# Gates of two token blocks written into a zeroed DRAM table by accumulating indirect DMAs, instead of through one-hot products

## The chip, the cores and the metric

One core of one Trainium2 chip runs the whole program. Its engines are TensorE (PE, with PEld for the weight load beside it), VectorE (DVE), ScalarE (ACT), GpSimd (POOL) and SyncE (SP). Plain DMAs are issued by SP, indirect ones by POOL. The metric is the device time of one execution in microseconds (us).

## The reference, cut to what matters

A decoder block over 1024 tokens of 1024 numbers, in float32: a gated DeltaNet and a sliding-window attention side by side, an output projection, a PEER layer (product-key retrieval of single-neuron experts), a gated input embedding and a last norm. The change is in the PEER layer. Each token and each of 8 heads picks 16 of 16,384 experts, with softmax gates:

```
qry = (ht @ wq).reshape(T, PEER_HEADS, 2, PEER_KEY_DIM)
sc = jnp.einsum("thpd,hpnd->thpn", qry, sub_keys)
top_s, top_i = lax.top_k(sc, K)                       # K = 16
cand_s = top_s[:, :, 0, :, None] + top_s[:, :, 1, None, :]
cand_i = top_i[:, :, 0, :, None] * PEER_N_KEYS + top_i[:, :, 1, None, :]
best_s, best_pos = lax.top_k(cand_s.reshape(T, PEER_HEADS, K * K), K)
expert = jnp.take_along_axis(cand_i.reshape(T, PEER_HEADS, K * K), best_pos, axis=-1)
gates = jax.nn.softmax(best_s, axis=-1)
act = jax.nn.gelu(jnp.einsum("td,thkd->thk", xb, u_tab[eb]))
y = jnp.einsum("thk,thkd->td", gb * act, v_tab[eb])
```

## The kernel before

The 1024 tokens are eight blocks of 128. Blocks 0 to 4 are computed densely: every expert's row of `u` and `v` passes through TensorE for all 640 tokens, and a table of gates (zero where an expert was not picked) multiplies the activations. Blocks 5 to 7 gather the picked rows instead: per block 128 indirect DMAs of 128 rows of 4 KB from `u` and 128 from `v` (L854), with a dot product or a multiply-add on VectorE for each.

`upstream()` (L325) comes first. `project` runs once for each half of the sequence (norm, input projection, convolution). Then, group by group of two blocks (`GROUPS`, L28), `mixers` computes DeltaNet and attention, and `retrieve` computes the output projection, the norm, the queries, the scores against the sub-keys, the first top-k (`first_topk`) and the second (`topk`). The norm's factor `rs` is computed by two small POOL instructions (`rs_v` L154, `rs` L155) that the norm on VectorE (`h<-x,rs,ffn_norm`) waits for; the DeltaNet output's factors `ro` and `rq` take the same two lines, and the attention's padded keys and values (`kz`, `vz`) are prepared on POOL too.

At the end of `topk` of a dense block, `gbuild` (L832) builds the block's part of the gate table: for four tokens at a time, VectorE compares an index row with `iota` twice (tiles `o1` and `o2`, shown as `o`), ScalarE scales by the gates, TensorE multiplies (`bk_gm`), ScalarE copies to `stage`, and 1 MB at a time goes to the DRAM table `gd` (L849), 40 stores in all. Every token block takes 64 one-hot comparisons.

`dense()` (L920) then takes the 128 rows of experts in groups of four (`cg`): it loads the group's gates into `Gt` (L965), multiplies the token parts by `u` (`bk_u`, parts of 320 + 320 tokens), applies Gelu, multiplies by the gates (`ge<-ge,Gt`), and sums the products with `v` (`bk_y`, `bk_yp`). Beside it a paced job issues the gathers of blocks 5 to 7, its VectorE work tied to the progress of the dense stage (`held_back`). `final()` ends the program. The pool `gp` of the gather buffers is opened at L352, inside `upstream`, the pool `gx` after it.

The order on each engine is set before the run, by a scheduler that simulates the program; on the chip each engine runs that order and waits where a semaphore says so. SP and POOL too issue their DMAs in that order.

Of the kernel before, what the change touches and what calls it, by code (L numbers as in the profile page):

```python
# [6 lines left out]

F32 = mybir.dt.float32
F32R = mybir.dt.float32r
BF = mybir.dt.bfloat16  # L10
I32 = mybir.dt.int32
# [18 lines left out]
DBLK = [0, 1, 2, 3, 4]  # L30
ABLK = [5, 6, 7]
# [3 lines left out]
GC = 4  # L35
# [10 lines left out]
def _consts():  # L46
    import numpy as np

    r = np.arange(P)
    parts = [np.eye(P), r[:, None] <= r[None, :], r[:, None] > r[None, :], np.ones((P, P)),  # L50
             np.broadcast_to(r[None, :], (P, P)), r[None, :] > r[:, None]]
    for l in range(7):
        s = 1 << l
        same = (r[:, None] // (2 * s)) == (r[None, :] // (2 * s))
        low = same & (r[:, None] % (2 * s) >= s) & (r[None, :] % (2 * s) < s)
        parts.append(low if l == 0 else low.T[:, r % (2 * s) >= s])
    sel = np.zeros((P, 8 + 50 + 16 + 16 + 16))
    sel[:, :8] = (500000.0 ** (-np.arange(0, 16, 2) / 16)).astype(np.float32)
    widths = [16 // (a + 1) for a in range(16)]
    starts = np.concatenate([[0], np.cumsum(widths)[:-1]])  # L60
    sel[:, 58:74] = starts
    sel[:, 74:90] = np.concatenate([[0], np.diff(starts)])
    sel[:, 90:106] = np.arange(16)
    return np.concatenate([np.concatenate(parts, axis=1), sel], axis=1).astype(np.float32)
# [3 lines left out]
def block_kernel(ctx: ExitStack, tc, I, out, dbg=None):  # L68
# [56 lines left out]
    negt = c2.tile([P, 1], F32, name="negt")  # L125

    def load_consts():
        nc.sync.dma_start(ident, I["consts"][:, 0:P])
        nc.sync.dma_start(cst, I["consts"][:, P:])
        V.tensor_copy(sel_b.rearrange("p s a h -> p (s a) h"), bc(sel[:, 58:106], 2, 8))  # L130
        V.memset(negt, NEG)

# [14 lines left out]
    gd = dr.tile([NE // GC, P, NT // TB, GC, TB], F32, name="gd")  # L147

    eidx = cp.tile([P, len(UBLK), P], I32, name="eidx")
# [71 lines left out]
    def project(hf, es):  # L221
# [30 lines left out]
        for ct in range(12):  # L252
            wh, wl = weights(I["wc"][ct], [P, DK, P])
            if hf:
                for i in range(2 * ct, 2 * ct + 2):
                    cached_tile(i)
            raw = sm.tile([P, 3 + H], F32, tag="craw", name="craw")
# [67 lines left out]
    def upstream():  # L325
        with early as em:
# [25 lines left out]
            pools["gp"] = ctx.enter_context(tc.tile_pool(name="gp", bufs=GBUF, side="right", reuse_waits="tile"))  # L352
# [29 lines left out]
    def retrieving(lt, es):  # L382
# [14 lines left out]
        def retrieve(gi):  # L397
# [62 lines left out]
            for bi, b in enumerate(grp):  # L460
                topk(lt, bg, b, tv[bi], tiu[bi])
                if b in HBLK:
                    pools["job"] = half_job()
                tick(2.0)

# [286 lines left out]
    def topk(tk, bg, b, v, iu):  # L752
# [52 lines left out]
        ga = gate_a[:, UBLK.index(b)] if b in UBLK else flat[:, 2 * P:3 * P]  # L805
# [9 lines left out]
        if b in ABLK:  # L815
            return
# [13 lines left out]
    slots = {}  # L830

    def gbuild(bg, b):  # L832
        tT = slots[b]
        for tb in range(P // TB):
# [14 lines left out]
            nc.sync.dma_start(gd[:, :, BBLK.index(b) * (P // TB) + tb].rearrange("g p c t -> p g (c t)"),  # L849
# [70 lines left out]
    def dense(xB):  # L920
        with ExitStack() as es:
# [12 lines left out]
            nparts = (NU + 511) // 512  # L934
            width = (NU // nparts + TB - 1) // TB * TB
            parts = [(n0, min(width, NU - n0)) for n0 in range(0, NU, width)]
# [26 lines left out]
            for cg in range(NE // GC):  # L963
                Gt = ap.tile([P, NT // TB, GC, TB], F32, tag="Gt", name="Gt", bufs=1)
                nc.sync.dma_start(Gt, gd[cg])  # L965
                vs, ws = [], []
                for ci in range(GC):
# [10 lines left out]
                    for n0, n in parts:  # L978
# [6 lines left out]
                        g3 = ge.rearrange("p (t k) -> p t k", k=TB)  # L985
                        m0 = NH + n0
                        tt(g3, g3, Gt[:, m0 // TB:(m0 + n) // TB, ci, :], ALU.mult)
# [76 lines left out]
    upstream()  # L1064
    pools["gx"] = ctx.enter_context(tc.tile_pool(name="gx", bufs=GXBUF, side="right", reuse_waits="tile"))
# [63 lines left out]
```

## Time and profile before

| | |
|---|---|
| median of 3 runs | 3067.3 us (3066.24 to 3071.76) |
| profiled execution | 3063.47 us |
| its span | 3061.7 us |
| mean granted TensorE clock | 0.982 |
| PE busy | 2943.6 us, 96% of the span |
| DVE busy | 2527.3 us, 83% |
| ACT busy | 1232.8 us, 40% |
| POOL busy | 1092.6 us, 36% |
| moved by DMA | 869.27 MB, mean 284 GB/s |

The profile shows busy time of each engine, and idle time with what ended it. Register and semaphore instructions and the issuing of plain DMAs are not counted as busy; an indirect DMA's issue on POOL is. "Landing" is the time from a DMA's issue to its last byte. Each row of a stage view tells busy time and number of instructions per engine, the granted clock as a share of full speed, and the mean share of the core's 16 DMA engines in use.

### The profile page before, as it was taken

The numbers are of one execution on the slowest core, as the hardware profiler recorded it, in microseconds if no ns is written. First come the engines' busy times: TensorE is split into PE (matmuls) and PEld (weight loads), VectorE is DVE, ScalarE is ACT, GpSimd is POOL, SyncE is SP. The second block draws the span as 40 slices with busy tenths as digits, with TensorE's granted clock in tenths as the row PEclk, the third lists the DMA queues.
The fourth block names the chain that finished last, engine by engine and source line by source line (L and its number), as shares of the span: only waits on it lengthen the run. The fifth ranks groups of instructions, "written<-read, shape, count | busy, mean of one in ns | idle before, by whom it ended". The sixth has DMA issues, their size and how long they took to land. (4 is left out here: it accounts for less than half of the span.)

```text
span 3061.7 us, 50184 instructions
## 1 busy us (share of the span) xinstructions
PE 2943.6 (96%) x18287; PEld 2694.2 (88%) x18287; DVE 2527.3 (83%) x5327; ACT 1232.8 (40%) x2761; POOL 1092.6 (36%) x901
## 2 busy tenths in 40 slices
PE   7999999999998877999999999999999999999998
PEld 5888999999997877889989989899899899998977
DVE  5658636899999879988899988889888888898984
ACT  5567634477876742322323223223222232222233
POOL 0000000000000001656465565655654665555631
PEclk9999999999999988999999999999999999999999
DMA  6569667778879895999899989989998899899962
GB/s 234 141 237 360 202 212 230 238 230 241 243 226 272 227 289 185 352 339 336 294 357 331 349 325 351 331 319 331 331 325 320 307 340 323 311 347 329 324 231 89
DMA packets 449815, 869.27 MB, mean 284 GB/s; under 512 B 193440, under 2 KB 235680, under 8 KB 445216
## 3 DMA queue, kind: packets, MB, share of 16 engines
q1 hardware_dynamic: 338976, 463.37, 45.6%
q0 software_dynamic: 110592, 402.70, 36.5%
q8 instruction: 144, 2.36, 0.3%
q14 instruction: 103, 0.84, 0.1%
HBM read 766.34 MB, written 99.61 MB: 283 GB/s over the span
## 5 line engine op out<-in xcount | busy, mean ns | idle before, releaser
L134 PE MATMUL bk_u<-hT,uh 128*128 128x320 f32 x4096 | 914.3, 310 | 8.6 <-DMA hT<-h2Td 6.5
L134 PEld LDWEIGHTS bk_u<-hT,uh 128*128 128x128 f32 x4096 | 694.5, 188 | 25.5 <-DMA hT<-h2Td 7.0
L854 POOL DMA_INDIRECT rows<-in_u_dram,eidx x384 | 516.7, 1346 | 539.6 <-DVE dots L864 328.4
L854 POOL DMA_INDIRECT rows<-in_v_dram,eidx x384 | 504.0, 1312 | 374.2 <-DVE acc L82 301.1
L134 PE MATMUL bk_u<-hT,ul 128*128 128x320 f32 x2048 | 634.1, 310 | 0.0
L82 DVE SCALAR_TENSOR_TENSOR acc<-rows,dots,acc 128x1024 f32<-128x1024 f32 x384 | 491.5, 1280 | 16.5 <-DMA rows<-in_v_dram,eidx 7.0
L864 DVE CUSTOM_DVE_ANT_0 rows<-rows,h2n 128x1024 f32<-128x1024 f32 x384 | 457.0, 1219 | 50.1 <-DMA rows<-in_u_dram,eidx 42.4
L134 PEld LDWEIGHTS bk_u<-hT,ul 128*128 128x128 f32 x2048 | 385.6, 188 | 3.3
L984 ACT ACTIVATE ge<-bk_u 128x320 f32<-128x320 f32 x256 | 109.4, 428 | 634.9 <-PE bk_u L134 610.2
L134 PE MATMUL bk_y<-vh,wh 128*128 128x512 f32 x768 | 301.6, 393 | 17.7 <-DVE xB L79 17.0
L134 PE MATMUL bk_y<-vl,wh 128*128 128x512 f32 x768 | 302.6, 394 | 0.0
L134 PE MATMUL bk_y<-vh,wl 128*128 128x512 f32 x768 | 301.0, 394 | 0.5 <-DVE wl L79 0.5
L76 ACT ACTIVATE wh<-ge 128x320 fp32r<-128x320 f32 x256 | 118.9, 469 | 308.4 <-DVE ge L79 270.2
L134 PE MATMUL bk_gm<-o,o 128*128 128x128 f32 x1280 | 203.2, 290 | 33.2 <-ACT o L76 21.0
L76 ACT ACTIVATE o<-o,tT 128x128 f32<-128x128 f32 x640 | 203.5, 392 | 57.9 <-DVE o L79 56.2
L134 PEld LDWEIGHTS bk_gm<-o,o 128*128 128x128 f32 x1280 | 179.5, 199 | 39.7 <-ACT o L76 26.0
L79 DVE TENSOR_TENSOR o<-cst,tT 128x512 f32<-128x512 f32 x320 | 204.7, 682 | 10.9 <-PE bk_gm L134 9.0
L134 PE MATMUL bk_s<-h,whi 128*128 128x256 f32 x1024 | 210.4, 297 | 2.9 <-DMA whi<-wqc 1.6
L76 ACT ACTIVATE vh<-vr 128x1024 fp32r<-128x1024 f32 x128 | 132.0, 1054 | 181.7 <-PE bk_y L134 100.5
L134 PE MATMUL bk_yp<-vh,wh 128*128 128x512 f32 x512 | 199.0, 392 | 2.2 <-ACT wh L76 2.2
L76 ACT ACTIVATE uh<-ur 128x1024 fp32r<-128x1024 f32 x128 | 135.3, 1057 | 160.4 <-PE bk_u L134 143.4
L134 PE MATMUL bk_yp<-vl,wh 128*128 128x512 f32 x512 | 199.5, 392 | 0.0
(302 smaller groups left out, 5861.8 us busy)
## 6 DMA issues: line engine op xcount, KB each, us to landing
ur<-in_uT_dram SPq DMA_DIRECT2D x128, 512.0 KB, 6.9
vr<-in_v_dram SPq DMA_DIRECT2D x128, 512.0 KB, 6.2
gd<-stage SPq DMA_DIRECT2D x40, 1024.0 KB, 7.0
Gt<-gd SPq DMA_DIRECT2D x32, 1280.0 KB, 8.8
wlo<-wqc SPq DMA_DIRECT2D x128, 256.0 KB, 4.4
whi<-wqc SPq DMA_DIRECT2D x128, 256.0 KB, 4.2
whi<-woc SPq DMA_DIRECT2D x64, 256.0 KB, 4.6
wlo<-woc SPq DMA_DIRECT2D x64, 256.0 KB, 4.8
```

The costliest lines, as they stand in the source:

```text
L76: return S.activation(o, i, AF.Copy, **k)
L79: return V.tensor_tensor(o, a, b, op)
L82: return V.scalar_tensor_tensor(o, a, s, b, op0, op1, **k)
L134: PE.matmul(o, l, r, start=start, stop=stop)
L854: G.indirect_dma_start(out=r, out_offset=None, in_=tab, in_offset=bass.IndirectOffsetOnAxis(ap=eidx[:, u, s:s + 1], axis=0))
L864: held_back(V.tensor_tensor_reduce(out=r, in0=r, in1=h2n, op0=ALU.mult, op1=ALU.add, scale=1.0, scalar=0.0, accum_out=dots[:, s:s + 1]))
L984: S.activation(ge, pa, AF.Gelu_apprx_tanh)
```

## The change

Blocks 0 and 1 (`SBLK`) no longer pass through `gbuild`. Their `topk` leaves the gates in `sgate` and an address in `sidx`: expert x 256 + token, the token counted within the two blocks. `scattered()`, called at the end of `retrieve(0)`, issues 8 x 2 x 16 = 256 indirect DMAs from POOL, each of which adds 128 gates (one for each token of a block) to 128 single elements of a second DRAM table, `gsd`, of 4,194,304 elements (16.8 MB). The 16 DMAs of a head carry a dependency on all 16 of the previous head of the same block, so that two heads that pick the same expert for the same token do not overlap. `gsd` is filled with zeros by 16 stores of 1 MB (2 KB pieces, from a zero tile in SBUF) that `project(0)` issues on SP. The table `gd` shrinks to the 384 tokens of blocks 2 to 4, with 24 stores instead of 40; in the dense stage a group loads `Gt` of 768 KB and `Gs` of 512 KB (in 1 KB pieces, from `gsd`) instead of `Gt` of 1280 KB, and the token parts become 256 + 384. The pool `gp` is opened after `upstream()`.

```diff
--- before
+++ after
@@ -28,6 +29,8 @@
 DBLK = [0, 1, 2, 3, 4]
+SBLK = [0, 1]
+NS = len(SBLK) * 128
 ABLK = [5, 6, 7]
@@ -58,6 +61,7 @@
     starts = np.concatenate([[0], np.cumsum(widths)[:-1]])
+    sel[:, 8] = r
     sel[:, 58:74] = starts
@@ -123,12 +127,17 @@
     negt = c2.tile([P, 1], F32, name="negt")
+    zero = c2.tile([P, 512], F32, name="zero")
+    scol = cp.tile([P, len(SBLK)], F32, name="scol")
...
         V.memset(negt, NEG)
+        V.memset(zero, 0.0)
+        for i in range(len(SBLK)):
+            V.tensor_scalar(scol[:, i:i + 1], sel[:, 8:9], float(i * P), None, op0=ALU.add)
@@ -144,8 +153,13 @@
     h2Td = [dr.tile([P, DK, NU], F32, name=f"h2Td{i}") for i in range(2)]
-    gd = dr.tile([NE // GC, P, NT // TB, GC, TB], F32, name="gd")
-
+    NO = NT - NS
+    gd = dr.tile([NE // GC, P, NO // TB, GC, TB], F32, name="gd")
+
+    gsd = dr.tile([NE * P * NS, 1], F32, name="gsd")
+    lanes = dram_disjoint_views(gsd, 16 * len(SBLK))
+    sidx = cp.tile([P, len(SBLK), P], I32, name="sidx")
+    sgate = cp.tile([P, len(SBLK), P], F32, name="sgate")
     eidx = cp.tile([P, len(UBLK), P], I32, name="eidx")
@@ -254,6 +268,10 @@
                     cached_tile(i)
+            if not hf and ct < 8:
+                for z in range(2 * ct, 2 * ct + 2):
+                    zf = gsd.rearrange("(z p n k) o -> z p n (k o)", z=16, p=P, k=512)[z]
+                    nc.sync.dma_start(zf, bc(zero, 1, zf.shape[1]))
             raw = sm.tile([P, 3 + H], F32, tag="craw", name="craw")
@@ -349,7 +367,6 @@
                 project(1, (c1, wp, sm))
-            pools["gp"] = ctx.enter_context(tc.tile_pool(name="gp", bufs=GBUF, side="right", reuse_waits="tile"))
             with ExitStack() as es:
@@ -459,9 +476,9 @@
                 topk(lt, bg, b, tv[bi], tiu[bi])
-                if b in HBLK:
-                    pools["job"] = half_job()
                 tick(2.0)
+            if any(b in SBLK for b in grp):
+                scattered([b for b in grp if b in SBLK])
@@ -802,7 +819,7 @@
-        ga = gate_a[:, UBLK.index(b)] if b in UBLK else flat[:, 2 * P:3 * P]
+        ga = gate_a[:, UBLK.index(b)] if b in UBLK else sgate[:, SBLK.index(b)] if b in SBLK else flat[:, 2 * P:3 * P]
         gv = ga.rearrange("p (h k) -> p h k", k=16)
@@ -812,7 +829,11 @@
             stt(eidx[:, UBLK.index(b)], i1, 128.0, i2, ALU.mult, ALU.add)
-        if b in ABLK:
+        if b in SBLK:
+            si = SBLK.index(b)
+            stt(i1, i1, 128.0, i2, ALU.mult, ALU.add)
+            V.tensor_scalar(sidx[:, si], i1, float(NS), scol[:, si:si + 1], op0=ALU.mult, op1=ALU.add)
+        if b in ABLK or b in SBLK:
             return
@@ -828,6 +849,25 @@
     slots = {}
+    sent = {}
+
+    def scattered(blocks):
+        for h in range(8):
+            for b in blocks:
+                si = SBLK.index(b)
+                now = []
+                for k in range(16):
+                    s = h * 16 + k
+                    i = G.indirect_dma_start(
+                        out=lanes[16 * si + k], out_offset=bass.IndirectOffsetOnAxis(ap=sidx[:, si, s:s + 1], axis=0),
+                        in_=sgate[:, si, s:s + 1], in_offset=None, compute_op=ALU.add)
+                    for j in sent.get(b, ()):
+                        tc.add_manual_dep(i.ins, j.name,
+                                          mybir.DependencyInfo(mybir.DependencyClass.Sync, mybir.DependencyReason.DATA),
+                                          reason="one head behind another")
+                    now.append(i.ins)
+                sent[b] = now
+
@@ -846,7 +886,7 @@
                 yield
-            nc.sync.dma_start(gd[:, :, BBLK.index(b) * (P // TB) + tb].rearrange("g p c t -> p g (c t)"),
+            nc.sync.dma_start(gd[:, :, (BBLK.index(b) - len(SBLK)) * (P // TB) + tb].rearrange("g p c t -> p g (c t)"),
                               stage.rearrange("p (g c) t -> p g (c t)", c=GC))
@@ -931,9 +971,7 @@
             nc.sync.dma_start(xB, x1d[BBLK[0]:BBLK[0] + NB].rearrange("b p d -> p b d"))
-            nparts = (NU + 511) // 512
-            width = (NU // nparts + TB - 1) // TB * TB
-            parts = [(n0, min(width, NU - n0)) for n0 in range(0, NU, width)]
+            parts = [(0, NS), (NS, NU - NS)]
             total = len(ABLK) * 2 * P
@@ -961,8 +999,10 @@
             for cg in range(NE // GC):
-                Gt = ap.tile([P, NT // TB, GC, TB], F32, tag="Gt", name="Gt", bufs=1)
+                Gt = ap.tile([P, NO // TB, GC, TB], F32, tag="Gt", name="Gt", bufs=1)
                 nc.sync.dma_start(Gt, gd[cg])
+                Gs = ap.tile([P, GC, NS], F32, tag="Gs", name="Gs", bufs=1)
+                nc.sync.dma_start(Gs, gsd.rearrange("(g c p t) o -> g p c (t o)", c=GC, p=P, t=NS)[cg])
                 vs, ws = [], []
@@ -982,9 +1022,12 @@
                         S.activation(ge, pa, AF.Gelu_apprx_tanh)
-                        g3 = ge.rearrange("p (t k) -> p t k", k=TB)
-                        m0 = NH + n0
-                        tt(g3, g3, Gt[:, m0 // TB:(m0 + n) // TB, ci, :], ALU.mult)
+                        m0 = n0
+                        if n0 == 0:
+                            tt(ge, ge, Gs[:, ci], ALU.mult)
+                        else:
+                            g3 = ge.rearrange("p (t k) -> p t k", k=TB)
+                            tt(g3, g3, Gt[:, :, ci, :], ALU.mult)
                         copy(wh[:, m0:m0 + n], ge)
@@ -1062,6 +1105,7 @@
     upstream()
+    pools["gp"] = ctx.enter_context(tc.tile_pool(name="gp", bufs=GBUF, side="right", reuse_waits="tile"))
     pools["gx"] = ctx.enter_context(tc.tile_pool(name="gx", bufs=GXBUF, side="right", reuse_waits="tile"))
...
         xB = xp.tile([P, NB, D], F32, name="xB")

```

Line numbers of the kernel after are 12 to 40 higher than before (`rs_v` is L168, `rs` L169, `kz` and `vz` L704 to L709, the gathers L894).

SP, from the first input tile on. Before (`wraw` weights, `xt` input tiles, `sinks` a small parameter, `prd` a product kept in DRAM):

```order
11 L202 DMA wraw<-in_pT_dram 128x2x512
12 L236 DMA xt<-in_x_dram 128x1024 x2
13 L202 DMA wraw<-in_wp_dram 128x2x512
14 L182 DMA sinks<-in_sinks_dram 128x8
15 L202 DMA wraw<-in_wp_dram 128x2x512
16 L219 DMA prd<-pr 128x512 x2
17 L236 DMA xt<-in_x_dram 128x1024
18 L202 DMA wraw<-in_wc_dram 128x1024
```

The same place on SP now; `gsd<-zero` is a store of zeros:

```order
12 L250 DMA xt<-in_x_dram 128x1024 x2
13 L216 DMA wraw<-in_wp_dram 128x2x512
14 L274 DMA gsd<-zero 512x1x512 x2
15 L216 DMA wraw<-in_wp_dram 128x2x512
16 L274 DMA gsd<-zero 512x1x512 x3
17 L233 DMA prd<-pr 128x512
18 L274 DMA gsd<-zero 512x1x512 x3
19 L233 DMA prd<-pr 128x512
20 L274 DMA gsd<-zero 512x1x512 x7
21 L250 DMA xt<-in_x_dram 128x1024
22 L274 DMA gsd<-zero 512x1x512
24 L216 DMA wraw<-in_wc_dram 128x1024
```

All 16 stores of zeros stand between the second and the fourth input tile, ahead of the first weight tile `in_wc`.

POOL, from the norms of blocks 2 and 3 (`rs` of one column) on. Before, with block 4's norm in the last two rows shown:

```order
70 L154 TENSOR_SCALAR rs_v<-ss 128x1
71 L155 TENSOR_TENSOR rs<-rs_v,mhalf 128x1
72 L692 COPY vz<-qk 128x64 x2
73 L154 TENSOR_SCALAR rs_v<-so 128x4
...
79 L154 TENSOR_SCALAR rs_v<-so 128x4
80 L155 TENSOR_TENSOR ro<-rs_v,mhalf 128x4
81 L154 TENSOR_SCALAR rs_v<-sq 128x8
82 L155 TENSOR_TENSOR rq<-rs_v,mhalf 128x8
83 L692 COPY vz<-qk 128x64 x2
84 L154 TENSOR_SCALAR rs_v<-ss 128x1
85 L155 TENSOR_TENSOR rs<-rs_v,mhalf 128x1
```

POOL now, from block 3's norm to block 4's; `gsd<-sgate,sidx` are the scatters:

```order
73 L169 TENSOR_TENSOR rs<-rs_v,mhalf 128x1
74 L861 DMA gsd<-sgate,sidx 4194304x1 x16
75 L168 TENSOR_SCALAR rs_v<-so 128x4
...
80 L861 DMA gsd<-sgate,sidx 4194304x1 x32
82 L861 DMA gsd<-sgate,sidx 4194304x1 x48
86 L861 DMA gsd<-sgate,sidx 4194304x1 x48
87 L169 TENSOR_TENSOR ro<-rs_v,mhalf 128x4
88 L169 TENSOR_TENSOR rq<-rs_v,mhalf 128x8
89 L861 DMA gsd<-sgate,sidx 4194304x1 x64
90 L168 TENSOR_SCALAR rs_v<-ss 128x1
91 L861 DMA gsd<-sgate,sidx 4194304x1 x48
93 L169 TENSOR_TENSOR rs<-rs_v,mhalf 128x1
```

Before, POOL has nothing but small arithmetic between the two norms. Now all 256 scatters stand between them (16 + 32 + 48 + 48 + 64 + 48), 144 of them ahead of the second `ro` and `rq` (block 5).

VectorE now, at block 3's norm; `sidx` is block 0's, the address that the first scatters wait for:

```order
751 L86 SCALAR_TENSOR_TENSOR h<-x_7242,rs,ffn_norm 128x1024
752 L83 TENSOR_TENSOR B<-A,cst 128x512
753 L835 TENSOR_SCALAR sidx<-cand,scol 128x128
754 L83 TENSOR_TENSOR qk<-rope 128x10x8 x2
755 L83 TENSOR_TENSOR aq<-bk_de,aq 128x512
```

The address of block 0 is ready two rows after that norm; block 1's stands some 130 rows further on.

## Rows read from the trace of the kernel before

**Rows 1.** The page, PE busy tenths in 40 slices of the span.

```profile
PE   7999999999998877999999999999999999999998
```

**Rows 2.** Windows by stage: us, busy time per engine (instructions), PEclk, DMA share, GB/s.

```profile
0.00:20.00 20.00, 7.91 (x25) 5.58 (x26) 10.03 (x31) 8.92 (x12) 2.78 (x15) 0.95 0.86 300
20.00:60.00 40.00, 33.62 (x134) 25.62 (x135) 20.46 (x31) 23.85 (x40) 4.43 (x9) 0.85 0.76 251
60.00:150.00 90.00, 90.00 (x516) 77.84 (x514) 59.84 (x103) 50.20 (x93) 2.59 (x4) 1.00 0.49 138
250.00:300.00 50.00, 46.77 (x290) 39.36 (x290) 42.56 (x76) 34.98 (x70) 1.12 (x4) 1.00 0.97 357
601.00:783.00 182.00, 179.16 (x1522) 175.13 (x1522) 174.28 (x688) 142.38 (x447) 11.00 (x16) 1.00 0.83 244
783.00:1136.00 353.00, 308.61 (x2376) 295.91 (x2376) 319.16 (x1165) 247.33 (x699) 12.13 (x16) 0.94 0.88 253
1250.00:2950.00 1700.00, 1694.81 (x9455) 1539.33 (x9453) 1482.81 (x2021) 445.08 (x731) 986.36 (x740) 1.00 0.91 330
```

**Rows 3.** Timelines of DVE and POOL at the norms of blocks 3 and 4.

```profile
600.90 1.27 DVE L82 SCALAR_TENSOR_TENSOR h<-x,rs,ffn_norm 128x1024 f32<-128x1024 f32 x1
...
778.73 0.19 POOL L154 TENSOR_SCALAR rs_v<-ss 128x1 f32<-128x1 f32 x1 [46.01 <-ACT h L188]
779.00 0.88 POOL L155 TENSOR_TENSOR rs<-rs_v,mhalf 128x1 f32<-128x1 f32 x1
...
783.06 1.27 DVE L82 SCALAR_TENSOR_TENSOR h<-x,rs,ffn_norm 128x1024 f32<-128x1024 f32 x1
```

**Rows 4.** Tile `sc`: duration min/median/max, first and last start.

```profile
L745 DVE MAX8 tv<-sc x128: 264/276/295, 485.6 to 1136.1; 128x8 f32<-128x128 f32 x128
```

**Rows 5.** Windows, tile `o` alone: PE, PEld, DVE, ACT.

```profile
601.00:783.00 182.00, 61.85 (x394) 54.03 (x394) 63.82 (x100) 63.71 (x200) 1.00 0.83 244
783.00:1136.00 353.00, 141.38 (x886) 125.50 (x886) 140.85 (x220) 139.81 (x440) 0.94 0.88 253
```

**Rows 6.** Tile `rows`, the gathers.

```profile
L854 POOL DMA_INDIRECT rows<-in_u_dram,eidx x384: 932/1247/2077, 1085.6 to 2654.2; - x192
...
L854 POOL DMA_INDIRECT rows<-in_v_dram,eidx x384: 932/1019/2489, 1445.9 to 2944.3; - x192
...
DMA to landing us min/median/max: 4.2/6.5/11.5
```

**Rows 7.** Timeline of POOL at the first gathers.

```profile
1087.09 0.94 POOL L854 DMA_INDIRECT rows<-in_u_dram,eidx  x1 [0.30 <-issue]
1088.34 1.12 POOL L854 DMA_INDIRECT rows<-in_u_dram,eidx  x1 [0.31 <-issue]
```

**Rows 8.** Lines of POOL, 1250 to 2950: busy, mean ns, idle before.

```profile
L854 POOL DMA_INDIRECT rows<-in_u_dram,eidx x354 | 480.7, 1358 | 337.9 <-DVE dots L864 245.0 <-issue 66.8 <-DVE acc L82 18.2
```

**Rows 9.** Timelines of PE in a projection and in the dense stage.

```profile
371.02 0.28 PE L134 MATMUL bk_acc<-whi,hTl 128*128 128x256 f32 x1
371.14 0.28 PE L134 MATMUL bk_acc<-whi,hTh 128*128 128x256 f32 x1
...
2000.10 0.39 PE L134 MATMUL bk_y<-vl,wh 128*128 128x512 f32 x1
2000.33 0.39 PE L134 MATMUL bk_y<-vh,wl 128*128 128x512 f32 x1
...
2001.39 0.46 PE L134 MATMUL bk_u<-hT,uh 128*128 128x320 f32 x2
...
2001.83 0.46 PE L134 MATMUL bk_u<-hT,uh 128*128 128x320 f32 x2
```

**Rows 10.** DMA issues: count, KB each, median us to landing.

```profile
gd<-stage SPq DMA_DIRECT2D x40, 1024.0 KB, 7.0
Gt<-gd SPq DMA_DIRECT2D x32, 1280.0 KB, 8.8
...
h2Td<-h SPq DMA_DIRECT2D x10, 512.0 KB, 5.5
```

More of the change, by code (lines that the diff above doesn't have):

```diff
@@ L6 @@
 from concourse._compat import with_exitstack
+from concourse.ap import dram_disjoint_views
 F32 = mybir.dt.float32
```

## The prediction

> **What bounds the kernel now.** I read the busy tenths of the page first, then the windows by stage, then the landmarks that end the stages, and last single lines and tiles. TensorE is busy nearly everywhere [rows 1]; the reader is to see in the windows where it is not. The first 60 us wait for inputs: PE works 7.91 of 20 and 33.62 of 40 us while the DMA engines are busy 0.86 and 0.76 of the time; from 60 us on PE works 90.00 of 90 us [rows 2]. From the norm of block 3 to the last first-stage maximum lie 535 us, in which VectorE is the fullest engine or next to it: 174.28 of 182 us up to the norm of block 4, 319.16 of 353 after it (PE 308.61) [rows 2]. The ends of that stretch are the norm of block 3 at 600.90, the norm of block 4 at 783.06, released by POOL's `rs` of 779.00 [rows 3], and the last `tv<-sc` at 1136.1 [rows 4]. Then the dense stage, PE 1694.81 of 1700 us, POOL 986.36, VectorE 1482.81 [rows 2]. So a microsecond gained before 1136 counts in full if nothing later gives it back, and a microsecond in which an engine of that stretch waits counts too.
>
> **What is removed.** One-hot products of blocks 0 and 1, which all lie in that stretch. Of the 320 VectorE operations that write one-hot tiles (100 + 220 [rows 5]), 128 go; one takes 63.82/100 = 0.64 us, so 82 us of VectorE and about two fifths of the ScalarE and PE work of those rows. What replaces it on VectorE per block is two small operations for `sidx`. The order lists also move rows: on VectorE the list between the norms of blocks 3 and 4 grows from 544 to 715 operations, with 126 one-hot ones instead of 100; from the norm of block 4 to the last `tv<-sc` it shrinks from 919 to 596, with 66 instead of 220. (An index search stands in the order as one row and in the trace as two, which does not alter the method, since each row is priced with its pair.) Other rows cost (174.28 - 63.82)/(544 - 100) = 0.249 us before and (319.16 - 140.85)/(919 - 220) = 0.255 us after the norm of block 4 [rows 2, 5]. The first part becomes 174.28 + 26 x 0.64 + 145 x 0.249 = 227 us, at the fullness it has now (0.957) 237 us. The second becomes 319.16 - 154 x 0.64 - 169 x 0.255 = 177.5 us, at its fullness (0.904) 196 us. If VectorE alone decided, 433 us would stand for 535: a gain of 102.
>
> **What is added there, on POOL.** 256 indirect DMAs of 128 single elements. POOL's order has all of them ahead of `rs` of block 4's norm, and 144 ahead of the last `ro` and `rq` of block 5. Behind `rs` waits the norm of block 4 on VectorE; behind that its transposes, the query products, the scores and all the top-k of blocks 4 and 5. So the time from the norm of block 3 to that of block 4 becomes the larger of 237 (VectorE) and 2 + 256 p + w, where 2 us is from the norm of block 3 to the index of block 0 (two VectorE rows behind it in the new order), p is the pitch of the scatters and w what they lose where a head waits until the previous one of its block has landed. The trace has no scatter; nearest are the gathers.
> - p: a gather occupies POOL at least 932 ns [rows 6], and from one POOL instruction to the next there can be 0.08 us (778.73 + 0.19 to 779.00 [rows 3]): 1.01 as lower bound. The fastest pitch of two gathers in a row is 0.94 + 0.31 = 1.25, since 0.30 "issue" stands ahead of each [rows 7]. The mean of a gather in the dense stage, 1.36 [rows 8], with that 0.30 gives 1.66 as upper bound of what gathers show. I take 1.40: VectorE is as busy as in the dense stage, but the source is one element a partition and not 4 KB.
> - w: most heads alternate between the two blocks, so the previous head of a block has had 16 pitches to land. In four places it has not (the second and third head of block 0, which go alone, and two of block 1). At the median landing of a gather, 6.5 us [rows 6], that is 26 us; at the shortest, 4.2, it is 17. In the new program the scatters share eight semaphores in turn, so each waits for the eighth before it: 8 x 1.40 = 11.2 us, which nearly every gather's landing meets (median 6.5, longest 11.5).
>
> 2 + 358 + 26 = 386, so POOL decides and not VectorE, which will sit idle some 150 us ahead of the norm of block 4. 386 + 196 = 582 against 535: **+47**. By p = 1.01 and w = 17 it would be 280 + 196 = 476, -59; by p = 1.66 it is 453 + 196 = 649, +114.
>
> The Trainium skill speaks of POOL's side here ("SBUF — State Buffer", section "🔬 SBUF: two separate sides"): while VectorE runs an operation in a two-port mode, GpSimd is locked out of the port pair through which it writes descriptors, so a DMA that it issues waits. The trace agrees that such an issue stretches: 932 to 2489 ns with the same bytes [rows 6], though it does not show why. If every scatter met the longest, p would be 2.79 and the time some 360 us above my sum; the median gather does not, so I keep 1.40.
>
> The same skill ("DMA: Bandwidth & Descriptors", section "Anatomy of one DMA — SWDGE (gpsimd) path") gives a fixed cost of about 2.0 us for such a DMA. By it w would be an estimated 8 us and the sum 18 us less. The shortest landing in this trace is 4.2 us [rows 6], so the measurement decides.
>
> **The zero fill.** 16 stores of 1 MB go into SP's queue ahead of the later `x` tiles and weights (the order list shows it). 16.8 MB at the best rate of a window, 357 GB/s [rows 2], are 47 us, at 300 GB/s 56. The first 60 us move 300 x 20 + 251 x 40 = 16.0 MB now; both together at 357 would need 92 us, that is 32 beyond the 60. PE has no slack afterwards to absorb it. Ends 32 and 56; I take the middle, **+44**.
>
> **Dense stage.** The token parts are 256 + 384 instead of 320 + 320. In a stream three 320-column products take 0.44 us (2001.39 to 2001.83), 0.147 each, and a 256-column one 0.12 [rows 9]: 0.46 and 0.47 ns a column, and the columns stay 640. 128 experts x 8 x 3 = 3072 pairs of products and a doubt of 0.003 us a pair make -9 to +9; I take 0. The gate reads: 768 KB in place of 1280 (8.8 us) and 512 KB more in 1 KB pieces (a 512 KB store of small pieces lands in 5.5) [rows 10], 14.3 us if one follows the other. They hide behind the value products of a group, 5 blocks x 2 x 4 experts x 3 = 120 of 0.23 us (2000.10 to 2000.33 [rows 9]), 27.6 us, as the load does now: 0. Without that cover it would be 32 x 5.5 = 176 us, which I hold for unlikely. 16 of the 40 `gd` stores go; they lie beside a busy PE: 0. The first gather goes at 1085.6 now, and 30 of the 384 of `u` lie ahead of 1250 [rows 6, 8]; opened late, the buffers come free later, and up to 22 dot products (some 26 us of VectorE at 1.2 each) move into the dense stage, where VectorE has 13% idle and POOL 42%. I put **+5** there (-10 to +25), a lower granted clock of PE beside its wait included (0.85 in the window from 20 to 60 us, where PE waits too [rows 2]).
>
> **Sum.** On the profiled execution, 3061.7 us of span in 3063.5: 3063.5 + 47 + 44 + 5 = **3160 us**. The median of the runs is 3067.3, so base and median differ by 4 us, which is inside the rounding of p.
>
> **Rivals.**
> 1. POOL keeps up (faster). A scatter carries 512 bytes, so it may cost POOL only the 1.01 us of the lower bound, or less. Then 476 + the rest gives 3063.5 - 59 + 44 + 5 = 3054; if VectorE decides, 3063.5 - 102 + 49 = 3010. It decides below p = 1.02 with w = 26, 1.06 with w = 17. For it: POOL works only 11.00 of 182 us in this stretch now [rows 2]. Against: no gather shows a pitch under 1.24.
> 2. The landing decides (much slower). An accumulation has to read what it adds to, here 128 single elements. If one lands in L > 8p, the eight semaphores set the pitch to L/8. For L = 15: 1.88 x 256 + 2 + 4 x 15 + 196 = 738, so 3063.5 + 203 + 49 = 3316; L = 20 gives some 3490; the upper bound of the gathers, p = 1.66, gives 3227. For it: gathers land in up to 11.5 us; against: their median is 6.5 with 512 KB each.
> 3. The zero fill is hidden: the queue runs it beside the inputs and PE finds its data in time: 3160 - 44 = 3116. For it: the DMA engines are idle 14 and 24% of the first windows; against: 24% of 40 and 14% of 20 are 12 us of 47.
>
> **Chances.** Forecast 0.5, rival 1 0.20, rival 2 0.17, rival 3 0.13. The range 3030 to 3320 takes in rival 3, the upper part of rival 1 and the lower of rival 2, and leaves out the rest, about 0.2. The forecast's own range is 3110 to 3230 (the ends of the zero fill and p from 1.25 to 1.66). What the measurement of this kernel can tell from no change is about 0.2%, 6 us. Faster by more holds nearly all of rival 1, 0.19; within it 0.05; slower 0.76.
>
> **What would show it.** In the first 70 us the stores of zeros beside an idle PE. On POOL the scatters at about 1.1 us busy and 0.3 between, and the norm of block 4 near 601 + 44 + 386 = 1031, released by POOL's `rs`, with VectorE and PE idle ahead of it and PE's granted clock down; the last `tv<-sc` near 1227; a dense stage as long as now. I am wrong if VectorE shows no idle time before that norm (rival 1), if scatters wait for landings of earlier ones throughout (rival 2), or if PE is as busy in the first 100 us as now (rival 3).

## The result, and the profile after

| | before | after |
|---|---|---|
| median | 3066.77 us (3061.9 to 3071.76) | 3349.12 us (3344.76 to 3354.71) |
| ratio | | 1.0921, 95% interval 1.0898 to 1.0944 |
| profiled execution: span, mean granted clock | 3061.7 us, 0.982 | 3350.7 us, 0.936 |

3160 us were predicted, with a range up to 3320: the direction was right, the size a third of what came. By the landmarks of [rows 3, 4] the 289 us of the two spans lie as follows.

| stretch | before | after | change | predicted |
|---|---|---|---|---|
| start to the norm of block 3 | 600.9 | 661.2 | +60.3 | +44 |
| norm of block 3 to that of block 4 | 182.2 | 506.9 | +324.7 | +204 |
| norm of block 4 to the last `tv<-sc` | 353.0 | 237.2 | -115.8 | -157 |
| from there to the end | 1925.6 | 1945.4 | +19.8 | +5 |

VectorE's timeline after, at the norms of blocks 3 and 4 (start, duration, operation, idle time ahead and what ended it), answers to [rows 3]:

```profile
661.18 1.28 DVE L86 SCALAR_TENSOR_TENSOR h<-x,rs,ffn_norm 128x1024 f32<-128x1024 f32 x1 [0.38 <-POOL rs L169]
...
949.44 1.12 DVE L86 SCALAR_TENSOR_TENSOR zs<-bk_dn,ro,zs 128x128 f32<-128x128 f32 x4 [106.76 <-POOL ro L169]
...
1168.11 1.28 DVE L86 SCALAR_TENSOR_TENSOR h<-x,rs,ffn_norm 128x1024 f32<-128x1024 f32 x1 [91.42 <-POOL rs L169]
```

VectorE stands still twice, 107 us for block 5's `ro` and 91 us for block 4's `rs`. Both are POOL's. POOL's timeline after, over the same stretch:

```profile
663.57 1.80 POOL L861 DMA_INDIRECT gsd<-sgate,sidx  x1 [2.42 <-DVE sidx L835]
665.67 1.58 POOL L861 DMA_INDIRECT gsd<-sgate,sidx  x1 [0.30 <-issue]
...
947.76 1.64 POOL L169 TENSOR_TENSOR ro<-rs_v,mhalf 128x4 f32<-128x4 f32 x1
...
1165.61 1.54 POOL L861 DMA_INDIRECT gsd<-sgate,sidx  x1 [0.30 <-issue]
...
1167.49 0.58 POOL L169 TENSOR_TENSOR rs<-rs_v,mhalf 128x1 f32<-128x1 f32 x1
```

The first scatter goes 2.4 us behind block 3's norm, the last 2 us ahead of block 4's `rs`; between them POOL does almost nothing else. The tile `gsd` after (duration min/median/max in ns, first and last start; then POOL's idle time before its instructions):

```profile
L861 POOL DMA_INDIRECT gsd<-sgate,sidx x256: 1536/1551/2801, 663.6 to 1165.6; - x128
L1005 SPq DMA_DIRECT2D Gs<-gsd x32: 360/377/387, 1418.2 to 3150.1; - x32
L274 SPq DMA_DIRECT2D gsd<-zero x16: 797/1616/2662, 11.9 to 53.0; - x16
its engine sat idle before it (us, times) until:
  issue: 76.7, 253
  DMA gsd<-sgate,sidx: 4.6, 2
```

A scatter holds POOL 1.55 us (median), and only 4.6 us in all went into waiting for landings. The shortest scatter is longer than the median gather of [rows 6]. The median landing of a scatter, where the trace tells it, is 3.1 us (the last number, in the view of DMA issues):

```profile
gsd<-sgate,sidx POOLq DMA_INDIRECT x256, 3.1
```

Some scatters take longer than the median. Lines of POOL (count, busy us, mean ns, idle before) from 760 to 860, where VectorE works 77 of 100 us, and from 860 to 950, where it works 0.6 of 90:

```profile
L861 POOL DMA_INDIRECT gsd<-sgate,sidx x50 | 84.9, 1698 | 15.1 <-issue 15.1
...
L861 POOL DMA_INDIRECT gsd<-sgate,sidx x48 | 74.6, 1555 | 14.6 <-issue 14.6
```

Over the whole trace, none of the 116 scatters with no VectorE work beside them took more than 1.60 us, and 53 of the other 140 did, the longest 2.80. These long ones add some 18 us to the 414 of all scatters. Stages after, which answer to [rows 2] (us, busy time of PE, PEld, DVE, ACT, POOL, then PEclk, DMA share, GB/s):

```profile
20.00:60.00 40.00, 9.08 (x26) 6.05 (x24) 6.23 (x17) 5.27 (x9) 0.88 (x1) 0.50 1.05 392
...
760.00:860.00 100.00, 48.21 (x275) 40.17 (x273) 77.32 (x339) 44.47 (x147) 85.00 (x55) 0.72 0.39 51
860.00:950.00 90.00, 0.16 (x1) 0.16 (x1) 0.56 (x3) 0.00 (x0) 75.68 (x50) 0.50 0.23 0
...
661.00:1168.00 507.00, 244.60 (x1760) 227.44 (x1760) 240.29 (x883) 182.03 (x559) 422.61 (x272) 0.74 0.52 94
1168.00:1405.00 237.00, 205.26 (x1569) 198.85 (x1569) 185.30 (x816) 95.79 (x250) 7.42 (x13) 0.91 0.83 261
1520.00:3220.00 1700.00, 1694.98 (x9401) 1527.62 (x9400) 1470.36 (x2010) 441.14 (x725) 968.93 (x737) 1.00 0.91 327
```

PE falls to 9 us of work in 40 while the zeros are stored; POOL is nearly the only engine at work in 860 to 950; the dense stage is as full as before.

### The profile page after: what moved, and what is told of

Read it like the earlier page. It is cut to its first block, busy times and chain, and to the rows that moved or that the text cites. A ratio compares the mean times of both kernels' runs of the same rounds, so it can differ in the third digit from the quotient of the medians.

```text
span 3350.7 us, 49084 instructions
## 1 busy us (share of the span) xinstructions
PE 2936.1 (88%) x17769; PEld 2661.2 (79%) x17769; DVE 2470.8 (74%) x5206; ACT 1123.6 (34%) x2437; POOL 1493.1 (45%) x1157
## 5 line engine op out<-in xcount | busy, mean ns | idle before, releaser
L143 PE MATMUL bk_u<-hT,uh 128*128 128x256 f32 (+1 forms) x4096 | 903.8, 310 | 11.5 <-DMA hT<-h2Td 7.2
L894 POOL DMA_INDIRECT rows<-in_u_dram,eidx x384 | 515.3, 1342 | 542.7 <-DVE dots L904 281.6
L894 POOL DMA_INDIRECT rows<-in_v_dram,eidx x384 | 497.4, 1295 | 373.7 <-DVE acc L86 311.3
L143 PE MATMUL bk_u<-hT,ul 128*128 128x256 f32 (+1 forms) x2048 | 633.8, 309 | 0.0
L861 POOL DMA_INDIRECT gsd<-sgate,sidx x256 | 414.4, 1619 | 83.7 <-issue 76.7
L1024 ACT ACTIVATE ge<-bk_u 128x256 f32<-128x256 f32 (+1 forms) x256 | 110.0, 430 | 587.4 <-PE bk_u L143 549.6
L143 PE MATMUL bk_s<-h,whi 128*128 128x256 f32 x1024 | 202.2, 294 | 6.8 <-DMA whi<-wqc 4.7
L80 ACT ACTIVATE wh<-ge 128x384 fp32r<-128x384 f32 (+1 forms) x256 | 117.7, 468 | 266.7 <-DVE ge L83 253.1
L83 DVE TENSOR_TENSOR ul<-ur,uh 128x1024 fp32r<-128x1024 f32 x128 | 156.3, 1221 | 57.2 <-ACT uh L80 57.0
L168 POOL TENSOR_SCALAR rs_v<-ss 128x1 f32<-128x1 f32 x32 | 10.0, 313 | 407.4 <-ACT h L202 397.5
L143 PE MATMUL bk_yp<-vh,wl 128*128 128x512 f32 x512 | 183.0, 395 | 0.0
```

The source lines that it names most:

```text
L80: return S.activation(o, i, AF.Copy, **k)
L83: return V.tensor_tensor(o, a, b, op)
L143: PE.matmul(o, l, r, start=start, stop=stop)
L168: G.tensor_scalar(v, src, scale, EPS, op0=ALU.mult, op1=ALU.add)
L861: i = G.indirect_dma_start(out=lanes[16 * si + k], out_offset=bass.IndirectOffsetOnAxis(ap=sidx[:, si, s:s + 1], axis=0), in_=sgate[:, si, ...
L894: G.indirect_dma_start(out=r, out_offset=None, in_=tab, in_offset=bass.IndirectOffsetOnAxis(ap=eidx[:, u, s:s + 1], axis=0))
```

## Experiments

Theory (POOL, later POSITION): the scatters cost what they cost because each holds POOL for long (price) and because the factors of the norms stand behind them in its order (place); the zero fill adds its own time. Rivals: the new order of the other engines (ORDER), landings, contention with the other engines (CONTENTION). The times of noscatter, half_heads and forms are of one execution each.

**The scatters left out.** Edit: the call of `scattered` goes.

> The kernel after without its 256 scatters (the gates of blocks 0 and 1 are left out; the zero fill, the reads of both tables and everything else stay). Theory POOL (the scatters stand in POOL's order ahead of the norm's factor): from the norm of block 3 to that of block 4 the 507 us fall to what VectorE needs, about 240; the 91 us and 107 us waits of VectorE for POOL go; the time is 3353 - 267 = about 3086. Rival ORDER (the wait comes from the new order of VectorE and PE and only shows at POOL): the stretch stays above 400 us and the time above 3250.

Measured: 3055.1 us, 294 under the kernel after. VectorE's timeline of this kernel at the two norms:

```profile
659.35 1.28 DVE L86 SCALAR_TENSOR_TENSOR h<-x,rs,ffn_norm 128x1024 f32<-128x1024 f32 x1 [0.38 <-POOL rs L169]
...
801.31 1.28 DVE L86 SCALAR_TENSOR_TENSOR h<-x,rs,ffn_norm 128x1024 f32<-128x1024 f32 x1
```

142 us lie between them and no wait for POOL ahead of the second. That is what theory POOL expects. It is less than the 240 that VectorE was thought to need, because the edit also changes VectorE's order: 599 of its instructions (122.9 us of work, no one-hot comparison) start between the two norms, against 883 (240.3 us, 126 comparisons) in the kernel after. So this run alone does not separate POOL from ORDER; plain_again below does. The last `tv<-sc` comes 473 us behind block 3's norm, 535 before the change.

**Half of the scatters.** `for h in range(8)` becomes `range(4)`.

> Scatters of heads 0 to 3 alone, 128 of 256 (the gates of heads 4 to 7 of blocks 0 and 1 are left out). Theory POOL with a fixed price each (1.54 busy and 0.30 between, 1.95 with all waits): the POOL path is 2 + 128 x 1.95 = 252 us against VectorE's 240, so nearly all of the 267 us go: about 3100. Rival LANDING (the price grows with the number in flight or the table's state): the pitch falls below 1.7 with fewer. Rival ORDER: above 3250.

Measured: 3170.6 us, 70 more than expected, at the same price each (median 1.543 us). POOL's timeline of this kernel:

```profile
880.55 1.62 POOL L169 TENSOR_TENSOR ro<-rs_v,mhalf 128x4 f32<-128x4 f32 x1
...
938.94 0.19 POOL L168 TENSOR_SCALAR rs_v<-ss 128x1 f32<-128x1 f32 x1 [21.40 <-ACT h L202]
```

All scatters were over at 917; block 4's `rs` then waited for its input. What decided is block 5's `ro` at 880, behind 112 scatters: from it DeltaNet and the output projection still take 60 us to the norm of block 4 (61 with no scatters: 740.2 to 801.3). So two waits stand one behind the other, and the prediction had only the last. They explain the stretch, 281 us for the 240 expected, which is 41 of the 70. The other 30 lie behind block 4's norm: to the first `bk_u` there are 268 us, against 236 in the kernel after, with 150 one-hot comparisons on VectorE up to the last `tv<-sc` instead of 66.

**Four kinds of indirect DMA with the same addresses.** Heads 0, 1 as before; 2, 3 without `compute_op`; 4, 5 `out=got[:, si, k:k + 1], in_=u` by single elements; 6, 7 from `u` by 4 elements.

> The 256 indirect DMAs in four kinds, one after the other: heads 0 and 1 accumulate as before, 2 and 3 write without accumulation, 4 and 5 gather single elements from the table u into SBUF, 6 and 7 gather 16 bytes each (all with the same addresses; the gates of heads 4 to 7 are left out, and heads that pick one expert for one token overwrite each other). What makes a scatter hold POOL 1.54 us where the fastest gather of 4 KB rows takes 0.94: theory ACCUMULATE: only heads 0 and 1 take 1.54, the rest about 1.0, time 3353 - 192 x 0.6 = 3238. Theory WRITE: the first 128 take 1.54, the gathers about 1.0, 3353 - 77 = 3276. Theory SMALL ELEMENTS: all four take 1.54, 3353; or the last kind alone is cheaper.

Measured: 3240.0 us. Lines of POOL of this kernel (count, busy us, mean ns, idle before):

```profile
L867 POOL DMA_INDIRECT gsd<-sgate,sidx x64 | 105.5, 1648 | 21.4 <-issue 18.8 <-DVE sidx L835 2.4 <-DVE tiu L767 0.2
L873 POOL DMA_INDIRECT wide<-in_u_dram,sidx x64 | 67.0, 1047 | 19.5 <-issue 19.5
L871 POOL DMA_INDIRECT got<-in_u_dram,sidx x64 | 64.7, 1011 | 19.4 <-issue 19.4
L869 POOL DMA_INDIRECT gsd<-sgate,sidx x64 | 64.3, 1005 | 23.3 <-issue 19.2 <-DMA gsd<-sgate,sidx 4.2
```

L867 accumulates, L869 writes the same elements without: 1.65 against 1.00 us. Direction and the size of what is moved (4 or 16 bytes) change nothing. Theory ACCUMULATE, on the number (3238).

**All scatters without accumulation.** `compute_op=ALU.add` goes.

> The kernel after with its 256 scatters written without accumulation, in the same places (where two heads pick one expert for one token, one gate is lost). By the four kinds a write holds POOL 0.96 us instead of 1.54, so the pitch falls from 1.85 to 1.26. Theory ACCUMULATE x POSITION (the prediction's sum was right but for the price of an accumulation): the POOL path from the norm of block 3 to that of block 4 is 2 + 256 x 1.26 + 30 = 355 us against 507, the time 3349 - 152 = 3197. Rival: the time is set by landings and the heads' order, then it stays above 3280.

The single execution of this run took 3380.4 us, with the engines in small steps that nothing in the profile explains. PE's and its loads' timeline of it:

```profile
784.46 0.29 PEld L143 LDWEIGHTS bk_s<-h,whi 128*128 128x128 f32 x1 [2.51 <-issue]
...
785.86 0.37 PE L143 MATMUL bk_s<-h,whi 128*128 128x256 f32 x1 [2.43 <-issue]
```

The same kernel in four more executions:

> The writes without accumulation once more, now in rounds: the one look gave 3380 where 3197 was expected, with VectorE, PE and ScalarE waiting for nothing that the profile shows, in steps of about 0.7 us. If that was one disturbed execution: 3197 (3170 to 3230). If plain writes of 4 bytes at a pitch of 1.26 us slow the other engines' work: again near 3380, and with the same steps in the trace.

Measured: 3202.1 us (3198.3 to 3203.4), ratio 1.0442 (1.0425 to 1.0458). Tile `gsd` of this execution:

```profile
L861 POOL DMA_INDIRECT gsd<-sgate,sidx x256: 955/962/3318, 663.2 to 1020.3; - x128
```

The norms of blocks 3 and 4 stand 361 us apart (660.8, 1022.2), by the sum 355. PE, VectorE, ScalarE and POOL run the same instructions in the same order as in the kernel after, so the 147 us that are gone are the accumulation's and not the order's: ORDER falls. With the pitch put right, the prediction's formula gives this stretch, but not the time: 3063.5 + (351 + 196 - 535) + 44 + 5 = 3125, 78 short. The expected 3197 started from the measured 3349, and so holds the other misses. The small steps did not come again; what slowed that one execution stays open.

**The zeros spread.** Each of the 16 stores waits for a VectorE result of a later convolution or projection tile (60 to 155 us) instead of standing in one row:

```diff
-            if not hf and ct < 8:
-                for z in range(2 * ct, 2 * ct + 2):
...
+            za = stt(acc, th, 1.0, acc, ALU.add, ALU.mult)
+            if not hf:
+                zeroed(ct, za)
```

> The kernel after with its 16 stores of zeros spread, one behind each convolution tile of the first half and four in the projection behind it (60 to 200 us, where the DMA engines were 0.41 to 0.55 busy before). Theory QUEUE (the fill costs what it costs because it stands in SP's order ahead of inputs, while there is room later): the norm of block 3 comes 43 to 60 us earlier, near 601 to 618, and the time is 3293 to 3310. Rival BANDWIDTH (16.8 MB more must be paid wherever they stand): the norm of block 3 stays near 650 and the time within 15 us of 3349.

Measured: 3304.95 us, ratio 1.0785 (1.0767 to 1.0803), 44 under the kernel after. Its tile `h`, and its windows in the order of the columns above:

```profile
L86 DVE SCALAR_TENSOR_TENSOR h<-xt,rs,mix_norm x8: 1276/1284/1286, 17.7 to 190.7; 128x1024 f32<-128x1024 f32 x8
```

```profile
20.00:60.00 40.00, 32.17 (x133) 24.04 (x132) 20.37 (x31) 24.42 (x41) 3.66 (x9) 0.91 0.76 250
60.00:100.00 40.00, 40.00 (x184) 32.42 (x183) 28.16 (x47) 21.40 (x32) 0.00 (x0) 1.00 0.78 255
100.00:150.00 50.00, 50.00 (x336) 45.55 (x335) 32.33 (x56) 25.51 (x42) 0.74 (x2) 1.00 1.01 337
```

The last `mix_norm` (the norm ahead of the second half's projection) starts at 190.7, as before the change (191.6), against 235.0 after: theory QUEUE. The DMA engines take the zeros beside a PE at work 90 of 90 us from 60 to 150.

**Both left out or spread.**

> The scatters left out (the gates of blocks 0 and 1 are missing) and the stores of zeros spread over 60 to 200 us. If the two costs add, 3055 - 44 = 3011: what the change would give if neither the fill nor the scatters cost anything, 53 under the kernel before. If the fill was partly hidden by the earlier end of the stretch, 3025 or more.

Measured: 3017.4 us, ratio 0.9843 (0.9824 to 0.9862). The two costs add (294 + 44 = 338 against 332), and the removed one-hot products are worth 48 us (3065.8 for the kernel before in the same series) where neither is paid.

**The gather buffers opened where they were**, without scatters.

> no_scatter_zero_spread (no scatters, so the gates of blocks 0 and 1 are missing) with the gather buffers opened where the kernel before opens them; the zero tile shrinks to 128 columns so that they fit, and its pieces to 512 bytes. In all kernels with the change the norm of block 3 comes 17 us later than before even where the zeros cost nothing (617.2 against 600.9). If the late buffers (the memory that other pools then get and wait for) do that: near 601 and 3000; if the order of the rest does: 617 and 3017.

Measured: 3029.1 us, ratio 0.9879 (0.9861 to 0.9896). Block 3's norm comes at 602.3 instead of 617.2, so the late buffers cost the 15 us there. (The zero tile and the pieces of its stores are smaller in this run too; their part was not taken apart.) The early buffers lose more later: the dense products of this kernel run from 1061.7 to 2912.4, those with late buffers from 1061.9 to 2884.1. The loss lies at the start: from 1061 to 1200 PE works 105 us at a granted clock of 0.85, with late buffers 132 at 0.96. What holds PE up there is open.

**The scatters spread over POOL's order**, zeros spread. Later heads go only behind POOL's factors of blocks 5, 6 and 7:

```diff
+    PLAN = {0: [0], 1: [1], 2: [2, 3], 3: [4], 4: [5, 6, 7]}
...
+        behind = pooled[-2:] if stage else []
```

> All 256 accumulating scatters, zeros spread, and the scatters cut into five parts of POOL's order: head 0 where it was, and the later heads only behind the factors ro of blocks 5, 6, 7 and rs of block 7. Nothing else changes. Theory POSITION (it is the place ahead of the factors that costs, not the scatters): no wait of VectorE for rs or ro above about 40 us, the last tv<-sc near 1130, then the dense stage waits for the last scatter, which POOL's own time sets: 618 + 2 + 256 x 1.85 + 30 + 20 = about 1145; time 3095 (3075 to 3130). Rival CONTENTION (256 scatters slow the other engines wherever they stand): above 3200.

Measured: 3188.1 us, ratio 1.0402 (1.0385 to 1.042). 117 us come back by place alone, but not all that was expected: each piece of 30 to 126 us still delays the next factor, so the last norm comes at 1068 (959 without scatters), and VectorE then waits 82 us for the first `Gs`, behind the last scatter at 1253.5.

**The same for block 0 alone.**

> As spread_two but for block 0 alone: 128 scatters, a table of 8.4 MB, 8 MB of zeros in pieces of half a megabyte, block 1 through the one-hot products as before, and the token parts 320 + 320 with two multiplications in the first. POOL has room for 128 x 1.95 = 250 us in 470. One block saves half of the 53 us that both save without costs, less some 8 us of VectorE for the added multiplication: theory POSITION gives 3040 to 3055, just under the kernel before (3064). If the added multiplication or the head-by-head waits decide, 3064 to 3090.

Measured: 3103.2 us, ratio 1.0123 (1.0103 to 1.0143): missed. Here too the pieces delay the factors (the last norm comes at 1068.6); a wait for `Gs` is not among VectorE's.

**Nothing but scatters on POOL.** The factors go to VectorE and ScalarE, zeros spread, scatters in one row as in the kernel after:

```diff
-        G.tensor_scalar(v, src, scale, EPS, op0=ALU.mult, op1=ALU.add)
-        G.tensor_tensor(dst, v, mhalf[:, 0:n], ALU.pow)
+        V.tensor_scalar(dst, src, scale, EPS, op0=ALU.mult, op1=ALU.add)
+        S.activation(dst, dst, AF.Sqrt)
+        V.reciprocal(dst, dst)
...
-        G.memset(kz, 0.0)
+        V.memset(kz, 0.0)
```

> Zeros spread, all 256 accumulating scatters as in the kernel after, but nothing else on POOL before the gathers: the factors rs, ro, rq are computed by VectorE and ScalarE (square root, reciprocal), and the padded keys and values are filled by VectorE. Theory POSITION: no wait of the norms; the norm of block 4 comes 140 to 180 us behind that of block 3 (507 in the kernel after); the scatters run through, 618 + 2 + 256 x 1.85 + 30 = 1124, and the dense stage, which could begin near 1065, waits for them: 3017 + 65 + 0 to 40 for the new factors = 3080 to 3125. Rival CONTENTION (scatters slow the other engines): the norm of block 4 more than 250 us behind that of block 3 and the time above 3180.

Measured: 3085.6 us, ratio 1.0072 (1.0052 to 1.0091). The norms of blocks 3 and 4 stand 139 us apart (627.0, 765.5). Tile `gsd`, and VectorE's waits (total, times, longest):

```profile
L868 POOL DMA_INDIRECT gsd<-sgate,sidx x256: 1546/1551/3737, 624.7 to 1139.4; - x128
```

```profile
DVE ge L83 <- DMA Gs<-gsd: 50.8, 1, 50.8
```

The same 256 scatters at the same price, with no factor behind them: 219 us gone against zero_spread. What is left is POOL's own time (the dense stage waits 51 us for the last scatter) and the price of the move. Theory POSITION; CONTENTION, which wanted more than 250 us between the norms, falls.

**The same for block 0 alone.**

> The same for block 0 alone (128 scatters, 8 MB of zeros, parts 320 + 320, block 1 by one-hot products). The scatters end near 618 + 2 + 128 x 1.85 + 35 = 892, far ahead of the dense stage, and no factor stands behind them. Theory POSITION: 3017 + 31 (the one-hot products of block 1) + 0 to 40 = 3048 to 3088, at or just under the kernel before; CONTENTION: 3100 or more, as spread_one.

Measured: 3055.7 us, ratio 0.9966 (0.9952 to 0.9979): under both kernels, by 0.3% under the one before. The same again:

> factors_off_pool_one once more beside it on the same chip: 3052 to 3060, ratio 0.995 to 0.998 to the kernel before.

Measured: 3056.4 us, 0.9972 (0.996 to 0.9984).

**Control: the factors moved in the kernel before.**

> The kernel before with the factors rs, ro, rq computed by VectorE and ScalarE and the padded keys and values filled by VectorE, as in factors_off_pool_one, and nothing else. If the 10 us that factors_off_pool_one lies under the kernel before come from the scatters of block 0: 3067 to 3090 (the new factors cost VectorE and ScalarE time and spare no wait, since POOL is nearly idle there). If they come from the factors' move: 3040 to 3058.

Measured: 3129.3 us, ratio 1.0207 (1.0191 to 1.0223), above both ranges. The move costs 66 us by itself, so the gain is not the move's. ScalarE loads its function table (ACT_TABLE_LOAD) 60 times here, 77.0 us in all, and 12 times, 15.4 us, in the kernel before. Whether that is the 66 us is not shown: factors_off_in_window_one below has 26 loads, factors_off_pool_one 62, at nearly the same time.

**The factors moved in the scatters' stretch alone**, for one block and for two (`off[0]` chooses the engine).

> factors_off_pool_one, but the factors stay on POOL except in the stretch in which the scatters run (norms of blocks 2 to 5, DeltaNet factors and padded keys of blocks 4 to 7). Moving all of them costs the kernel before 66 us (3129 against 3064). If that price is paid evenly by the 8 blocks of each kind, about half comes back: 3056 - 30 = 3025 (3010 to 3045). If it is paid in this very stretch: 3050 to 3060.

> The same with both blocks scattered (256 scatters; the factors stay on POOL but for the norms of blocks 2 to 7, the DeltaNet factors and padded keys of blocks 4 to 7, and later). POOL's own time bounds it: the scatters end no earlier than 618 + 2 + 256 x 1.85 + 30 = 1124 and the dense stage waits for them: 3070 to 3090, not under the kernel before.

Measured: 3053.4 us, 0.9965 (0.9952 to 0.9979), and 3090.5 us, 1.0089 (1.0074 to 1.0105). For one block this is the fastest of all complete versions, level with factors_off_pool_one: to leave the other factors on POOL gains 2 to 3 us and not the 30 of an even price. For two blocks VectorE again waits 52 us for `Gs`: POOL's time is the bound.

## Why the prediction was wrong

- **The step that failed** is the pitch: "I take 1.40", with "1.66 as upper bound of what gathers show". The 256 scatters took 414.4 us busy and 76.7 of issue, 1.92 each: 133 us more than the sum had, of the 193 by which the span missed. All bounds came from gathers, which do not accumulate. The accumulation is what costs: without it the same 256 took 269.4 us busy and 76.5 of issue (plain_again), 1.35 each, near the 1.40. Rival 1 and the upper end left it out; rival 2 looked for its price in the landing, and it stands in POOL's own busy time. The path itself was right: POOL's `rs` behind all scatters released the norm of block 4, with VectorE and PE idle ahead of it.
- **The heads' waits for landings**, put at four of 6.5 us, 26 in all, were two, of 4.6 in all: the scatters land in 3.1 us, not in the 6.5 of 4 KB rows. Other work of POOL was 9 us. So 133 - 21 + 9 = 121, which is the first stretch's excess. The 2.0 us that the Trainium skill gives ("DMA: Bandwidth & Descriptors", section "Anatomy of one DMA — SWDGE (gpsimd) path") would have made 8, nearer to the 4.6; as a landing it is too short here, where the shortest in the tile's view is 2.9.
- **The second stretch** was priced by VectorE alone, 177.5 us at a fullness of 0.904. VectorE worked 185.3 us, but at 0.78: 41 us. PE works 205 of the 237. From 1180 to 1200 alone, behind the norm, VectorE works 1.7 us while PE works 18.5; before the change 220 one-hot comparisons lay in this stretch, now 66. PE starts at a granted clock of 0.50, after 88 us without work, but is back at 1.00 in the window from 1175 to 1180; over the stretch it has 0.91, against 0.94 before, which makes only a few of the 41. The same stretch takes 236 us in plain_again; no run takes its causes apart.
- **One path of two.** The prediction took the larger of VectorE's work and the scatters up to `rs`. Block 5's `ro` and the 60 us behind it are another path, hidden in the kernel after, decisive with half of the scatters.
- **The zero fill** came out as predicted: 43 us at the last `mix_norm`, 44 by zero_spread, predicted 44. The queue was right; that the middle of 32 and 56 hit so closely is luck. (At the 392 GB/s of the window from 20 to 60 us, 16.8 MB take 43 us.) The other 16 us ahead of block 3's norm are mostly the late buffers (15 in buffers_early), which the prediction had looked for behind the upstream part only.
- **The dense stage** was right: first `bk_u` to last `bk_y` 1829.7 us against 1821.5. Of the +19.8 another 7 lie ahead of it and 4 behind, 15 more than the +5 in all. The four misses, 121, 41, 16 and 15, make up the 193.
- **Rivals.** Rival 1 falls with the two waits of VectorE for POOL. Rival 2 gave a time nearer to the measured one (3316), but not its mechanism: nearly no scatter waited for a landing. Rival 3 falls by the 43 us and by zero_spread.
- **Scatters beside VectorE.** The median price does not depend on it, the long scatters do: 1698 ns in the mean beside a VectorE busy 77 us of 100, 1555 beside an idle one, some 18 of the 133 us. The Trainium skill has a rule that VectorE's work in a two-port mode keeps GpSimd from writing descriptors ("SBUF — State Buffer", section "🔬 SBUF: two separate sides"). The trace agrees in direction, but it does not show the lock, and the rule does not explain the 1.55 us, which stand beside an idle VectorE too.

## What to carry to other kernels

Before an operation goes to an engine that is nearly idle, look at what stands behind it in that engine's order: here small operations, 11 us of POOL's work between the two norms before the change, decided over 219 of the 288 us that the scatters cost with the zeros spread (zero_spread, no_scatter_zero_spread, factors_off_pool_two, the move's own price included). A price is read from an operation of the same kind; bounds from neighbours do not hold for what the neighbour does not do (here: accumulate). A fill of a table costs its place in the queue, not its bytes, as long as some later stretch has room.

## What the runs showed of the hardware

An accumulating indirect DMA of 128 single elements holds POOL 1.55 us, the same one without accumulation 0.96; gathers of 4 and of 16 bytes take 0.95 (medians), like those of 4 KB rows at their fastest (0.93). The next one starts 0.30 us later. The median does not depend on the number of scatters (1.543 at 128, 1.551 at 256). In the kernel after, no scatter beside an idle VectorE took over 1.60 us; beside a working one some took up to 2.80. While the zeros were stored, PE's granted clock fell to 0.50 with 9 us of work in 40 (1.2 GHz of 2.4), and was back at 1.00 in the window from 100 us on.
